# Two hybrid decoder layers on one core: planned weight conversions, attention in equal rounds from the second query slab on, a split last unit

## The chip, the cores and the metric

The kernel runs on one core of a Trainium2 chip. The metric is the device time of one execution in microseconds (us); lower is better. The engines are named as the profile names them: PE (TensorE matmul), PEld (its weight loads), DVE (VectorE), ACT (ScalarE), POOL (GpSimd), SP (SyncE, which issues nearly all DMAs).

## The reference

512 tokens of 1024 features go through two layers. Each layer projects the normalised tokens into an HGRN2 group (a gated linear recurrence, 8 heads) and a sliding-window attention group (16 query heads of 64, 2 key/value heads, window 128), and projects the joined, gated outputs back:

```python
def hybrid_layer(x, w_in, w_out, g_pre, g_post, lb, g_head, sinks):
    h = rms_norm(x, g_pre)
    proj = jnp.einsum('bsd,de->bse', h, w_in)
    q_h, f_h, i_h, z_h, q_a, k_a, v_a, z_a = jnp.split(proj, SPLIT_POINTS, axis=-1)
    o_h = hgrn2(q_h, f_h, i_h, lb)
    o_h = rms_norm(o_h, g_head).reshape(B, S, HG_WIDTH).astype(z_h.dtype) * jax.nn.silu(z_h)
    q_a = rotary(q_a.reshape(B, S, ATT_HEADS, ATT_HEAD_DIM), pos)
    k_a = rotary(k_a.reshape(B, S, ATT_KV_HEADS, ATT_HEAD_DIM), pos)
    o_a = sliding_window_attention(q_a, k_a, v_a, sinks).astype(z_a.dtype) * jax.nn.silu(z_a)
    y = jnp.einsum('bse,ed->bsd', jnp.concatenate([o_h, o_a], axis=-1), w_out)
    return x + rms_norm(y, g_post)
```

Attention works on blocks of 128 queries, each with its own and the previous block of keys, with a causal band of 128, a learned sink per head in the softmax, and rotated queries and keys. All data are float32.

## The kernel before

**Projections.** Every projection is made of three fp32r products of split operands (high x low, low x high, high x high), so each weight piece of 128 x 512 is converted after its load: ACT rounds it to `whi` (line 177), DVE, for some pieces POOL, subtracts that from it into `wlo` (line 178). Eight pieces make a *slab*. The slabs of a layer come in a fixed order: kv, two query slabs (QA), two of HGRN2's inputs (IV), then FQ (forget gates and queries), ZA (attention's gate), the output parts a0 and a1, FQ again, and so on to ZH, h0 and h1. Raw pieces have 4 buffers, converted ones 9 (`RAW_BUFS`, `W_BUFS`).

**Units and steps.** A slab is worked off in *units*, one output tile in the PSUM tag `pj` (3 buffers) each: four units of eight steps for an input slab, eight of four steps for an output part. A step is three matmuls of 128 x 512 (line 240). `step()` starts the next unit when none is active or the active one is half done, and then alternates between the two. When a unit starts, `w_conv` writes down the conversions of its whole slab; after each step it writes down as many pieces of the next slab as the step's share of this slab, and four more (`LEAD`). In the QA, FQ and ZA slabs a unit needs two of the eight pieces, in the others all eight.

**What sets the order.** `merge` interleaves a stream of other work with `step()` by shares of their totals; the scheduler of the tile framework then orders each engine's instructions by their dependences, by free buffers and by the place in the program. On the chip each engine runs its list in order.

**Attention.** A step of attention is a group of four heads (g = 0 to 3) and a block of queries (n = 0 to 3), 16 steps in all. `att_scores` needs one PSUM bank for n = 0 and two for the others out of three (`sc`, taken in turn): scores on PE (lines 474, 485), masking copy and maximum on DVE (477 to 490), `negm` and `ds` (493, 495), four exponentials on ACT that free the bank (499), sum and reciprocal on DVE, scaling on POOL (506). `att_transpose` follows two steps later (PE line 512, split on ACT and DVE, two selects on POOL, line 524), `att_value` four steps later (PE line 538, ACT 540, DVE 544). Each of the three counts 1 in `merge`, of a total of 50, against the 96 steps of IV, IV + 1 and the first FQ slab. It begins when all four groups of queries are there and two more steps are done.

**Queries.** `qa_stream` rotates a group on DVE (435 to 442) and POOL (445, 446), splits it (448, 449), writes it to DRAM (`stack`, line 451) and reads it back stacked (`qs`, four DMAs, line 454) into one of two buffers, all issued from SP, as the raw weight loads are.

**The end of a layer.** After each row tile's two units of h1, `final` adds up (776), squares (805), scales (807 on POOL, 810 on DVE), takes the root (296, 298) and adds the residual (813), and stores (814).

Of the kernel before, what the change touches and what calls it, by code (L numbers as in the profile page):

```python
# [19 lines left out]
DEPTH = 2  # L20
# [9 lines left out]
QA, IV, FQ, ZA, ZH = 0, 2, 4, 8, 10  # L30

# [3 lines left out]
VLAG = 4  # L35
DEFER = 18
PJ, SC = 3, 3
LEAD = 4
# [27 lines left out]
def hybrid_kernel(ctx: ExitStack, tc: tile.TileContext, x, wkv, win, wout, g_pre, g_post, lbp, ghead, sinks,  # L66
# [78 lines left out]
    ahead = {("kv", l): sum(slab_first["out", l - 1, "h1"]) for l in range(1, DEPTH)}  # L145
    for l in range(DEPTH - 1):
        ahead["out", l, "h1"] = sum(slab_first["out", l, "h1"]) - KT - LEAD
# [61 lines left out]
    class Unit:  # L209
        def __init__(self, key, ks, sta, mov, evac, needs, ncol):  # L210
            self.key, self.ks, self.sta, self.mov, self.evac, self.needs, self.ncol = key, list(ks), sta, mov, evac, needs, ncol
            self.i = 0
            self.fresh = key[0] == "kv"
            self.list = products(self.ks, self.fresh)

    units, active, turn, slab_steps, slab_done = deque(), [], [0], {}, {}

    def enqueue(key, specs, ncol=512):

        for ks, sta, mov, evac, needs in specs:  # L220
            units.append(Unit(key, ks, sta, mov, evac, needs, ncol))
            slab_steps[key] = slab_steps.get(key, 0) + len(units[-1].ks)
            slab_done.setdefault(key, 0)

    def step():
        if not active or (len(active) == 1 and units and not active[0].fresh and not units[0].fresh
                          and 2 * (len(active[0].ks) - active[0].i) <= len(active[0].ks)):
# [9 lines left out]
        turn[0] += 1  # L237
        for n in range(3 * u.i, 3 * u.i + 3):
# [8 lines left out]
        first, n = slab_first[u.key]  # L247
        w_conv(ahead.get(u.key, first + n) + slab_done[u.key] * KT // slab_steps[u.key] + LEAD)
# [125 lines left out]
    def layer(l, last):  # L374
# [51 lines left out]
        qs = {}  # L426

        def qa_stream(s):
            hold = {}

            def evac(m, o):
# [20 lines left out]
                st = big.tile([P, 4, 512], F32R, tag="b8", name="qs", bufs=2)  # L452
                for row, j, i in ((0, 1, 0), (32, 0, 1), (64, 0, 0), (96, 1, 1)):
                    nc.sync.dma_start(st[row:row + 32].bitcast(F32), stack[j, i].rearrange("(h p) t -> p h t", h=4))
                qs[g] = st
# [90 lines left out]
        def att_stream(steps):  # L546
            pts, terms = {}, {}
# [3 lines left out]
            for i in range(n + VLAG):  # L551
                if i < n:
                    until(lambda: steps[i][0] in qs)
                    pts[i] = att_scores(*steps[i])
                    yield 1.0
                if 2 <= i <= n + 1:
                    terms[i - 2] = att_transpose(*steps[i - 2], pts.pop(i - 2), i % 2)
                    yield 1.0
                if i >= VLAG:
                    att_value(*steps[i - VLAG], terms.pop(i - VLAG))  # L560
                    yield 1.0
# [206 lines left out]
        def wo_stream(b, s, final=None):  # L768
            def evac(o, tt, ch):
# [4 lines left out]
                else:  # L774
                    with tc.high_priority(200 if final else 0):
                        nc.vector.tensor_tensor(yt[tt][:, ch], o, yt[tt][:, ch], op=ALU.add)
                if final is not None:
                    final(tt, ch)

            enqueue(("out", l, f"{b}{s}"),  # L780
                    [(range(4 * ch, 4 * ch + 4), lambda k, w, tt=tt: tuple(t[:, k % 4, tt * P:(tt + 1) * P] for t in ops_t[b, s]),
                      lambda k, w: w[k], lambda o, tt=tt, ch=ch: evac(o, tt, ch), [("o", l, b, s, tt)])
                     for tt, ch in ([(tt, ch) for tt in range(NT) for ch in range(2)] if final else
# [245 lines left out]
```

## Time and profile before

| | us |
|---|---|
| median of three runs | 943.63 (943.48 to 945.7) |
| the profiled execution | 947.07 |
| its span | 945.3 |
| PE busy | 915.7 |
| DVE busy | 678.3 |
| ACT busy | 471.6 |
| POOL busy | 269.1 |

The span runs from the first instruction to the last; the execution's own time holds the launch beside it. In a row of instructions, the first two numbers are start and duration in us, then engine, line, operation, output<-inputs and shape; the bracket at the end is how long the engine stood idle before it, and what ended that. Matmul ends are modelled, so the pitch from start to start says more than a duration. In layer 0 attention runs from 75 us to 184 us, in layer 1 from 540 to 650; layer 1 begins at about 485.

### The profile page before, as it was taken

Reading aid. Unit: us, or ns where it says so; the run is one execution under the profiler, and the core shown is the slowest. Engines: PE = TensorE matmul, PEld = TensorE weight load, DVE = VectorE, ACT = ScalarE, POOL = GpSimd, SP = SyncE. Lnnn points to the kernel's source line nnn. Section 1 sums busy time; section 2 is a strip of 40 time slices with the busy share of each in tenths; the row PEclk is TensorE's granted clock in tenths of the full one; section 3 lists DMA queues with packets and bytes.
Section 4 is the critical chain, followed back from the end, with each engine's and each line's share of the span. In section 5 each row is a group of like instructions: output and inputs, shape, how many; then the busy total and the mean of one; then the engine's idle time right before and its main releaser. Section 6 shows DMA issues by size and latency. Waiting matters only on the chain.

```text
span 945.3 us, 19028 instructions
## 1 busy us (share of the span) xinstructions
PE 915.7 (97%) x7228; PEld 754.0 (80%) x7228; DVE 678.3 (72%) x1320; ACT 471.6 (50%) x1099; POOL 269.1 (28%) x287
## 2 busy tenths in 40 slices
PE   8999998999999999999989989989999999999996
PEld 6887887778878888788878878877787887887885
DVE  5886878786676784855787677878867677749446
ACT  4534766837364462434453266675463635425242
POOL 2423443422231221311232244432413213113102
PEclk9999999999999999999999999999999999999998
DMA  6475522222222232323356735222222233322313
GB/s 218 153 232 147 170 49 87 67 80 68 79 84 85 82 111 88 117 86 104 120 162 184 222 71 164 68 61 85 69 67 91 68 90 111 102 68 92 89 34 133
DMA packets 56427, 100.75 MB, mean 107 GB/s; under 512 B 6544, under 2 KB 8848, under 8 KB 56336
## 3 DMA queue, kind: packets, MB, share of 16 engines
q1 hardware_dynamic: 56048, 99.27, 34.9%
q8 instruction: 57, 0.93, 0.4%
q10 hardware_dynamic: 288, 0.27, 0.1%
q14 instruction: 34, 0.28, 0.1%
HBM read 86.93 MB, written 12.58 MB: 105 GB/s over the span
## 4 chain that ended last, share of the span: by engine, by line
PE 77%; DVE 9%; ACT 6%; issue 5%; POOL 2%; DMA 1%; DVEq 0%; POOLq 0%; SPq 0%; ACTq 0%
PE pj L240 64%; DVE wlo L178 3%; PE sc L640 2%; ACT s L499 2%; PE sc L485 2%; PE ac L709 2%; PE ac L697 1%; PE ac L538 1%; PE ac L712 1%; ACT whi L177 1%; DVE oa L544 1%; PE sc L757 1%; DVE mx L490 1%; PE sc L512 1%; PE sc L687 1%
## 5 line engine op out<-in xcount | busy, mean ns | idle before, releaser
L177 ACT CAST whi<-raw 128x512 fp32r<-128x512 f32 x256 | 157.8, 620 | 179.8 <-PE pj L240 159.8
L178 DVE TENSOR_TENSOR wlo<-raw,whi 128x512 fp32r<-128x512 f32 x249 | 189.0, 765 | 55.4 <-ACT whi L177 53.7
L240 PE MATMUL pj<-hhi,wlo 128*128 128x512 f32 x512 | 205.5, 401 | 0.0
L240 PE MATMUL pj<-hhi,whi 128*128 128x512 f32 x512 | 200.2, 391 | 0.0
L240 PE MATMUL pj<-hlo,whi 128*128 128x512 f32 x512 | 200.0, 391 | 0.0
L240 PE MATMUL pj<-whi,ops 128*128 128x512 f32 x512 | 173.5, 398 | 0.0
L240 PEld LDWEIGHTS pj<-hhi,whi 128*128 128x128 f32 x512 | 96.2, 188 | 20.9
L240 PEld LDWEIGHTS pj<-whi,ops 128*128 128x128 f32 x512 | 96.2, 188 | 19.9
L240 PEld LDWEIGHTS pj<-hhi,wlo 128*128 128x128 f32 x512 | 96.3, 188 | 19.0
L240 PEld LDWEIGHTS pj<-hlo,whi 128*128 128x128 f32 x512 | 96.5, 189 | 18.3
L240 PE MATMUL pj<-whi,hlo 128*128 128x512 f32 x256 | 104.6, 408 | 0.0
L240 PE MATMUL pj<-whi,hhi 128*128 128x512 f32 x256 | 101.0, 395 | 0.0
L240 PE MATMUL pj<-wlo,hhi 128*128 128x512 f32 x256 | 100.9, 394 | 0.0
L240 PE MATMUL pj<-wlo,ops 128*128 128x512 f32 x256 | 99.8, 390 | 0.0
L658 POOL TENSOR_TENSOR k<-k,tot 128x256 f32<-128x256 f32 x80 | 65.3, 835 | 109.6 <-PE sc L640 64.1
L657 DVE TENSOR_TENSOR q<-q,tot 128x256 f32<-128x256 f32 x80 | 48.2, 630 | 15.6 <-PE sc L640 10.1
L499 ACT ACTIVATE s<-sc,negm 128x128 f32<-128x128 f32 x128 | 45.6, 369 | 24.6 <-DVE negm L493 22.5
L240 PEld LDWEIGHTS pj<-whi,hhi 128*128 128x128 f32 x256 | 48.5, 189 | 10.2
L506 POOL TENSOR_TENSOR s<-s,sums 128x512 f32<-128x512 f32 x32 | 33.4, 1043 | 78.0 <-DVE sums L504 39.3
L240 PEld LDWEIGHTS pj<-wlo,ops 128*128 128x128 f32 x256 | 48.2, 188 | 8.9
L240 PEld LDWEIGHTS pj<-whi,hlo 128*128 128x128 f32 x256 | 48.6, 190 | 8.1
L240 PEld LDWEIGHTS pj<-wlo,hhi 128*128 128x128 f32 x256 | 48.7, 190 | 7.8
(182 smaller groups left out, 1431.5 us busy)
## 6 DMA issues: line engine op xcount, KB each, us to landing
raw<-in_win_dram SPq DMA_DIRECT2D x192, 256.0 KB, 2.7
raw<-in_wout_dram SPq DMA_DIRECT2D x64, 256.0 KB, 2.7
stack<-rot SPq DMA_DIRECT2D x16, 512.0 KB, 4.1
qs<-stack SPq DMA_DIRECT2D x32, 256.0 KB, 4.7
a<-in_x_dram SPq DMA_DIRECT2D x11, 256.0 KB, 3.6
raw<-in_wkv_dram SPq DMA_DIRECT2D x8, 256.0 KB, 4.0
x_mid<-a SPq DMA_DIRECT2D x8, 256.0 KB, 2.2
a<-x_mid SPq DMA_DIRECT2D x8, 256.0 KB, 3.0
```

The costliest lines, as they stand in the source:

```text
L177: keep(nc.scalar.copy(hi, v))
L178: keep((nc.gpsimd if i in on_pool and i % 2 else nc.vector).tensor_tensor(lo, v, hi.bitcast(F32), op=ALU.subtract))
L240: nc.tensor.matmul(u.o, lhsT=u.sta(k, u.w)[i], rhs=u.mov(k, u.w)[j], start=(n == 0), stop=(n == len(u.list) - 1))
L485: pin(nc.tensor.matmul(S[:, h * 256:(h + 1) * 256], lhsT=q[:, 2 * hp_ + h, t_], rhs=kst[v][p][:, (n - 1) * P:(n + 1) * P], start=(h == 0 a ...
L490: nc.vector.tensor_reduce(mx_[:, 2 * hp_:2 * hp_ + 2], Sv[:, :, P:2 * P], axis=AX.X, op=ALU.max)
L499: nc.scalar.activation(pt[:, h * P:(h + 1) * P], cur[h], AF.Exp, bias=negm[:, h:h + 1], scale=SCALE, accum_out=sums[:, h:h + 1])
L506: nc.gpsimd.tensor_tensor(pv, pv, sums.unsqueeze(2).broadcast_to([P, 4, P]), op=ALU.mult)
L512: pin(nc.tensor.transpose(T[:, h * P:(h + 1) * P], pt[:, h * P:(h + 1) * P], ident))
L640: pin(nc.tensor.matmul(L[32 * b:32 * b + 32, c:c + 16], lhsT=k[:, o_:o_ + 32], rhs=qv[:, blk:blk + qu, 1, :], start=True, stop=True, tile_ ...
L657: nc.vector.tensor_tensor(qv[:, :, 1, :], qv[:, :, 1, :], tv[:, :, 0].unsqueeze(2).broadcast_to([P, nb, hh]), op=ALU.mult)
L658: nc.gpsimd.tensor_tensor(kv_[:, :, 0, :], kv_[:, :, 0, :], tv[:, :, 1].unsqueeze(2).broadcast_to([P, nb, hh]), op=ALU.mult)
L709: pin(nc.tensor.matmul(O[:, c], lhsT=A[:, c], rhs=vs(j, n), start=(n == 0), stop=False))
```

## The change

- `plan_conversions` runs through all units once before the first step and notes at which step each weight piece is first used. Each piece is due 14 steps before that (`LEAD`), and at least 3 steps before the next piece (`SPACE`); `step()` writes down a conversion when it is due, or when a unit's step needs it. Nothing else is written down at a unit's start, and a step asks for its own pieces alone.
- Attention starts when two groups of queries are there and eight more steps are done (`QWAIT`), in the second QA slab. Its total is now 20, one for each round, and the one to three pieces of a round share that 1. The steps set against it are what is left of the second QA slab, IV, IV + 1 and the first FQ slab.
- The stacked queries of groups 2 and 3 are read back after the last score step of groups 0 and 1.
- The units of the last layer's h1 are not interleaved. Its last unit is split in two of 256 columns each, with its own sums, and the last row tile's stores go out in three parts, one of them from ACT's queue.

```diff
+    def begins(active, units):
+        return not active or (len(active) == 1 and units and not active[0].alone and not units[0].alone
+                              and 2 * (len(active[0].ks) - active[0].i) <= len(active[0].ks))
+    def plan_conversions():
+        first, on, rest, n = {}, [], deque(units), 0
+        while on or rest:
+            if begins(on, rest):
+                on.append(rest.popleft())
+            u = on[n % len(on)]
+            for j in u.pieces if u.fresh else [u.pieces[u.i]]:
+                first.setdefault(slab_first[u.key][0] + j, n)
...
+        for p in reversed(range(len(pieces))):
+            late = min(late, first[p] - LEAD) if p not in kv_pieces else late
+            due.insert(0, late)
+            late -= SPACE
...
     def step():
...
             u = units.popleft()
-            first, n = slab_first[u.key]
-            w_conv(first + n)
-            u.w = [conv[first + j] for j in range(n)]
...
+        for j in u.pieces if u.fresh else [u.pieces[u.i]]:
+            w_conv(first + j + 1)
+            u.w[j] = conv[first + j]
...
-        w_conv(ahead.get(u.key, first + n) + slab_done[u.key] * KT // slab_steps[u.key] + LEAD)
+        while state["conv"] < len(pieces) and due[state["conv"]] <= turn[0]:
+            n = state["conv"]
+            w_conv(n + 1)
+            if state["conv"] == n:
+                break
...
+        def load_q(g):
+            st = big.tile([P, 4, 512], F32R, tag="b8", name="qs", bufs=2)
+            for row, j, i in ((0, 1, 0), (32, 0, 1), (64, 0, 0), (96, 1, 1)):
+                nc.sync.dma_start(st[row:row + 32].bitcast(F32), stacks[g][j, i].rearrange("(h p) t -> p h t", h=4))
+            qs[g] = st
...
+                stacks[g] = stack
+                if g < 2:
+                    load_q(g)
...
             for i in range(n + VLAG):
+                todo = []
                 if i < n:
-                    until(lambda: steps[i][0] in qs)
-                    pts[i] = att_scores(*steps[i])
-                    yield 1.0
+                    todo.append(lambda: pts.update({i: att_scores(*steps[i])}))
...
+                for fn in todo:
+                    fn()
+                    yield 1.0 / len(todo)
+                if i < n and steps[i][1] == NT - 1 and steps[i][0] < 2:
+                    until(lambda: steps[i][0] + 2 in stacks)
+                    load_q(steps[i][0] + 2)
...
+                if last:
+                    todo[-1:] = [(NT - 1, 1, 0, 256), (NT - 1, 1, 256, 256)]
...
-            until(lambda: 3 in qs)
-            for _ in range(2):
+            until(lambda: 1 in qs)
+            for _ in range(QWAIT):
                 step()
-            merge((att_stream([(g, n) for g in range(4) for n in range(NT)]), 50), rest(("in", l, FQ)))
+            merge((att_stream([(g, n) for g in range(4) for n in range(NT)]), 4 * NT + VLAG), rest(("in", l, FQ)))
```

How the instructions stand, at three places. **PE, the first score steps of layer 0** (`sc` are the three banks, `ident,s` is the transpose of the first step). Before, with six, six, three and three projection matmuls at the gaps:

```order
L474 MATMUL sc_80<-kst,qs 128x128 x8
...
L485 MATMUL sc_78<-kst,qs 128x256 x4
L485 MATMUL sc_79<-kst,qs 128x256 x4
...
L485 MATMUL sc_80<-kst,qs 128x256 x4
...
L485 MATMUL sc_78<-kst,qs 128x256 x4
...
L512 MATMUL sc_79<-ident,s 128x128 x4
```

Now, with 18, three and six at the gaps:

```order
L520 MATMUL sc_80<-kst,qs 128x128 x8
L531 MATMUL sc_78<-kst,qs 128x256 x4
L531 MATMUL sc_79<-kst,qs 128x256 x4
...
L531 MATMUL sc_80<-kst,qs 128x256 x4
...
L531 MATMUL sc_78<-kst,qs 128x256 x4
...
L558 MATMUL sc_79<-ident,s 128x128 x4
```

The third step, which takes bank 80 again, stands 18 projection matmuls behind the second instead of six. The first stands 60 of them earlier in the program: 51 matmuls into the second QA slab, where before it stood 15 into IV. In both orders later steps are 18 matmuls apart.

**DVE, where the second QA slab ends and IV begins in layer 0** (`rot<-pj` are the rotations of the slab's last unit). Now:

```order
L325 TENSOR_TENSOR a<-sc_79,a 128x512
L488 TENSOR_TENSOR rot<-pj,cs 128x512
L177 TENSOR_TENSOR wlo<-raw,whi 128x512 x3
L489 TENSOR_TENSOR rot<-pj,cs 128x512
L177 TENSOR_TENSOR wlo<-raw,whi 128x512
L496 TENSOR_TENSOR rot<-rot 128x512
L523 COPY_PREDICATED sc_80<-masks,neg 128x512
```

Before:

```order
L178 TENSOR_TENSOR wlo<-raw,whi 128x512
L441 TENSOR_TENSOR rot<-pj,cs 128x512
L442 TENSOR_TENSOR rot<-pj,cs 128x512
L449 TENSOR_TENSOR rot<-rot 128x512 x2
L477 COPY_PREDICATED sc_80<-masks,neg 128x512
```

Before, all eight pieces of IV were converted ahead of the last rotation; now the fourth and later ones stand behind it, and four score steps stand ahead of it.

**DVE, a score step near the end of attention in layer 0** (from the masking copies to `negm`, on which the exponentials wait). Before, the 14th step, at the start of FQ:

```order
L544 TENSOR_TENSOR oa<-ac,u 64x2x128 x2
L178 TENSOR_TENSOR wlo<-raw,whi 128x512
L489 COPY_PREDICATED sc_80<-masks,sc_80 128x2x128
L489 COPY_PREDICATED sc_78<-masks,sc_78 128x2x128
L490 TENSOR_REDUCE mx<-sc_80 128x2
L178 TENSOR_TENSOR wlo<-raw,whi 128x512
L490 TENSOR_REDUCE mx<-sc_78 128x2
L284 TENSOR_TENSOR a<-sc_79,a 128x512
L178 TENSOR_TENSOR wlo<-raw,whi 128x512
L493 SCALAR_TENSOR_TENSOR negm<-mx,nsnk 128x4
```

Now, the 15th, at the end of IV + 1:

```order
L590 TENSOR_TENSOR oa<-ac,u 64x2x128 x2
L535 COPY_PREDICATED sc_80<-masks,sc_80 128x2x128
L535 COPY_PREDICATED sc_78<-masks,sc_78 128x2x128
L536 TENSOR_REDUCE mx<-sc_80 128x2
L536 TENSOR_REDUCE mx<-sc_78 128x2
L177 TENSOR_TENSOR wlo<-raw,whi 128x512
L539 SCALAR_TENSOR_TENSOR negm<-mx,nsnk 128x4
```

One conversion is left in this chain where there were three. Before, the last score step stands 36 matmuls into FQ, now nine. ACT's list has 18 table loads instead of 22.

More of the change, by code (lines that the diff above doesn't have):

```diff
@@ L35 @@
 VLAG = 4
+QWAIT = 8
 DEFER = 18
 PJ, SC = 3, 3
-LEAD = 4
+LEAD, SPACE = 14, 3
 POOL_SLABS = (QA,)
@@ L225, in step @@
     def step():
-        if not active or (len(active) == 1 and units and not active[0].fresh and not units[0].fresh
-                          and 2 * (len(active[0].ks) - active[0].i) <= len(active[0].ks)):
+        if not due:
+            plan_conversions()
+        if begins(active, units):
             u = units.popleft()
-            first, n = slab_first[u.key]
-            w_conv(first + n)
-            u.w = [conv[first + j] for j in range(n)]
             for key in u.needs:
```

84 lines of the change are left out of this document (55 added, 29 removed).

## The prediction

> **What bounds the kernel now.** I read the page first, then the table of waits of the tensor engine, then busy time by stage, then the timeline of single stalls.
>
> ```profile
> span 945.3 us, 19028 instructions
> PE 915.7 (97%) x7228; PEld 754.0 (80%) x7228; DVE 678.3 (72%) x1320; ACT 471.6 (50%) x1099; POOL 269.1 (28%) x287
> ```
>
> The tensor engine (PE) is busy for 97% of the span, and the change adds twelve matmuls and removes none. So it can only win back PE's idle time, time at a reduced clock, and what follows the last matmul. Of the waits, one is large:
>
> ```profile
> PE sc L485 <- ACT s L499: 11.5, 11, 2.6
> ```
>
> The score matmuls of attention (line 485) wait for the exponentials (line 499) that free one of the three score banks. By stage (columns: stretch, its length, then busy us and count of PE, PEld, DVE, ACT, POOL, then PE's granted clock, DMA share, GB/s), three stretches of each layer hold most of it:
>
> ```profile
> 75.00:90.00 15.00, 12.98 (x68) 10.91 (x67) 10.54 (x29) 7.52 (x32) 4.77 (x5) 0.89 0.25 95
> 90.00:105.00 15.00, 14.58 (x82) 12.12 (x81) 12.82 (x29) 9.74 (x36) 9.35 (x9) 1.00 0.55 149
> 150.00:165.00 15.00, 12.45 (x67) 10.29 (x66) 13.02 (x31) 9.65 (x30) 4.88 (x5) 1.00 0.23 73
> 540.00:555.00 15.00, 12.83 (x64) 10.73 (x63) 11.46 (x32) 8.67 (x33) 3.52 (x4) 0.89 0.12 44
> 555.00:570.00 15.00, 14.33 (x76) 11.51 (x75) 13.15 (x28) 10.50 (x37) 9.03 (x9) 1.00 0.63 169
> 615.00:630.00 15.00, 12.46 (x61) 10.43 (x60) 11.66 (x29) 8.43 (x27) 4.61 (x4) 0.89 0.24 71
> ```
>
> Length less PE busy is the idle time: at attention's start 2.02 + 0.42 us in layer 0 and 2.17 + 0.67 in layer 1, near its end 2.55 and 2.54. Three of the stretches show a clock of 0.89: 15 us x 0.11 = 1.65 us lost at most; since part of the slow time falls into the stall itself I take 1.4 each.
>
> **Start of attention.** What ended the first stall, with PE's pitch ahead of it:
>
> ```profile
> 77.66 1.12 PE L485 MATMUL sc<-kst,qs 128*128 128x256 f32 x8
> 78.61 0.40 PE L240 MATMUL pj<-whi,hlo 128*128 128x512 f32 x1
> ...
> 79.55 0.39 PE L240 MATMUL pj<-wlo,hhi 128*128 128x512 f32 x1
> 79.78 0.39 PE L240 MATMUL pj<-whi,hhi 128*128 128x512 f32 x1
> 82.18 0.51 PE L485 MATMUL sc<-kst,qs 128*128 128x256 f32 x2 [2.02 <-ACT s L499]
> ```
>
> Projection matmuls follow each other every 0.23 us; eight score matmuls take 78.61 - 77.66 = 0.95. The third score step comes six projection matmuls after the second, too soon for the exponentials of the first. The order after the change puts 18 there: twelve more, 12 x 0.23 = 2.8 us, over the 2.02 and 2.17 that were missing. So this stall and its slow clock should go: 2.02 + 0.42 + 1.4 = 3.8 in layer 0, 2.17 + 0.67 + 1.4 = 4.2 in layer 1, 8.1 in all.
>
> But attention now starts inside the second query slab, where VectorE (DVE) also rotates queries. From the first score to that slab's end, PE has 54 projection matmuls x 0.23 = 12.4 us, four score steps at 0.95 and two transposes of half the columns of a score step at about 0.4: 17 us. DVE's work there, counted in its new order, by these groups (line, op, count, total us, mean ns) of the attention stage of layer 0, and a rotation and a conversion ahead of it:
>
> ```profile
> L284 DVE TENSOR_TENSOR a<-sc,a 128x512 fp32r<-128x512 f32 x16 | 11.0, 686 | 1.1 <-ACT a L283 0.5
> L489 DVE COPY_PREDICATED sc<-masks,sc 128x256 f32<-128x256 uint8 x24 | 9.7, 422 | 3.7 <-PE sc L485 1.5 <-ACT a L283 1.1 <-ACT whi L177 0.9
> L490 DVE TENSOR_REDUCE mx<-sc 128x2 f32<-128x256 f32 x24 | 9.6, 418 | 0.2
> L503 DVE TENSOR_TENSOR sums<-sums,es 128x4 f32<-128x4 f32 x16 | 5.5, 341 | 9.5 <-ACT es L502 9.5
> ```
>
> ```profile
> 63.93 0.68 DVE L442 TENSOR_TENSOR rot<-pj,cs 128x512 f32<-128x512 f32 x1
> 64.53 1.41 DVE L178 TENSOR_TENSOR wlo<-raw,whi 128x512 fp32r<-128x512 f32 x1
> ```
>
> Eight masking copies and eight maxima (the full-width one as two) 8 x (0.42 + 0.42) = 6.7; sixteen small ones at up to 0.34, 5.4; two transposed subtracts 1.4; four rotations 2.7; two rounding subtracts of that width and one conversion at up to 1.41, 4.2: 20.4 us. With the small ones at 0.15, as line 296 below, and those three at 0.68, it is 15.2. DVE is thus as full as PE. The next slab's fourth and later conversions stand behind the last rotation in DVE's queue, and PE's first unit of IV waits for them. The lower count gives PE no stall; the upper, (20.4 + 0.95 until the first score is there - 17) + rotation 0.68 + conversion 0.68 - (0.95 + 0.23 of PE work ahead of it), a stall of 4.5. I take 1.5 per layer, below the middle, since the group means lie nearer to their short ends. **Term A: -8.1 + 3.0 = -5.1, ends +0.9 and -8.1.**
>
> The DMAs move too:
>
> ```profile
> 51.54 1.27 SPq L454 DMA_DIRECT2D qs<-stack  x3
> ...
> 72.78 0.99 SPq L157 DMA_DIRECT2D raw<-in_win_dram  x1
> 89.40 1.75 SPq L454 DMA_DIRECT2D qs<-stack  x4
> ```
>
> SP stands from 73.8 to 89.4 on the read-back of the third stack, since both buffers are in use, with the raw weight loads behind it. The change issues that read-back when its buffer is nearly free. PE shows no wait for a weight there, so I cost the gain at nothing. The first score needs the first stack's read-back:
>
> ```profile
> 75.36 0.33 PE L474 MATMUL sc<-kst,qs 128*128 128x128 f32 x2
> ```
>
> ```profile
> qs<-stack SPq DMA_DIRECT2D x32, 256.0 KB, 4.7
> ```
>
> That score moves ahead by 60 projection matmuls, 13.8 us, to 61.6; the last part of the read-back, issued by 52.8, lands 4.7 later at 57.5. The 4 us between hide it; without them PE would wait for what is missing, at most one landing.
>
> **End of attention.** The second stall of layer 0, the conversions that DVE did in the 4 us ahead of it (count, shortest, median and longest in ns, first and last start), and a table load:
>
> ```profile
> 155.81 0.73 PE L485 MATMUL sc<-kst,qs 128*128 128x256 f32 x4 [2.56 <-ACT s L499]
> ```
>
> ```profile
> L178 DVE TENSOR_TENSOR wlo<-raw,whi x3: 676/676/996, 149.8 to 153.3; 128x512 fp32r<-128x512 f32 x3
> ```
>
> ```profile
> 161.32 1.28 ACT L583 ACT_TABLE_LOAD   x1
> ```
>
> Here the eight weight pieces of the first FQ slab are converted at once, three of them inside the chain copy, maximum, negm on which the exponentials wait: 0.68 + 0.68 + 1.00. In the new order one is left, so the chain is shorter by 1.7 of the 2.55. The scores also end 9 matmuls into FQ instead of 36, and four loads of the exponential or sigmoid table go, 4 x 1.28 us of ScalarE, which is off PE's path except here. I take -1.7 in layer 0 and -1.7 - 1.4 (the slow clock) in layer 1. **Term B: -4.8, ends 0 and -6.5** (2.55 + 2.54 + 1.4).
>
> **The tail.** DVE behind PE's last matmul:
>
> ```profile
> 936.60 0.69 DVE L776 TENSOR_TENSOR y<-pj,y 128x512 f32<-128x512 f32 x1 [0.27 <-PE pj L240]
> 937.33 1.71 DVE L810 TENSOR_TENSOR s<-y,b 128x512 f32<-128x512 f32 x1
> 938.96 0.15 DVE L296 SCALAR_TENSOR_TENSOR s<-ss 128x1 f32<-128x1 f32 x1
> 939.76 0.75 DVE L813 SCALAR_TENSOR_TENSOR a<-y,r,a 128x512 f32<-128x512 f32 x1 [0.66 <-POOL r L298]
> 940.43 0.74 DVE L813 SCALAR_TENSOR_TENSOR a<-s,r,a 128x512 f32<-128x512 f32 x1
> ```
>
> From 936.60, when PE's last matmul is done, to DVE's last end, 941.17, is 4.6 us. Now half a unit comes last, at about 0.42 for a half-width operation (line 490's size): y 0.4, square and its sum on ScalarE about 0.6, then 0.15 and the 0.8 to line 813, then 0.67 + 2 x 0.42: 3.3 us. The multiply of line 810, drawn out to 1.71 beside POOL's, is no longer there at the end, since the units now run one after the other and the first half-row is done 2.7 us earlier. Against it, 24 matmuls of 256 columns at 0.95 / 8 = 0.119 in place of 12 at 0.23 cost 0.1. **Term C: -1.2, ends -0.5 and -1.5.** The rest, the conversions shifted elsewhere and the seam between the layers: 0, plus or minus 1.5: no wait of PE there is in the table beside the one above, and the conversions run under PE's matmuls on engines that are busy for 72% and 50%; without that cover each would cost PE its 0.68.
>
> Sum: -5.1 - 4.8 - 1.2 = -11.1. The profiled execution took 947.07 us with a span of 945.3; the span would be 934.2. The median of the runs, 943.63, lies below that execution, and against it I predict **932.5 us**.
>
> **Two rules against the change.** The rotation's POOL part began just ahead of the conversion quoted above, and this stood beside POOL's selects:
>
> ```profile
> 64.09 1.29 POOL L445 TENSOR_TENSOR rot<-rot 128x512 f32<-128x512 f32 x1 [7.41 <-DVE rot L441]
> ```
>
> ```profile
> 153.87 1.04 DVE L493 SCALAR_TENSOR_TENSOR negm<-mx,nsnk 128x4 f32<-128x4 f32 x1
> ```
>
> The conversion took 1.41 instead of 0.68, and negm 1.04, where line 296 took 0.15 for as much. The Trainium skill, page "SBUF — State Buffer", section "Who interferes with whom", says why: a VectorE instruction with two SBUF inputs and a GpSimd one that reads SBUF exclude each other for the whole instruction. By that rule attention beside the rotations is worse than either alone; the case is the slower rival below. The clock: the Trainium skill, page "TensorE: Matmul & The Clock Gate", section "What's actually happening", halves it after an idle window of about 3.4 us; by that the three slow stretches would not exist, and the sum would be -6.9. Here 2.02 us sufficed, and the stall of 2.56 ahead of 155.81 did not: the windows' 0.89 and 1.00 decide.
>
> **Rivals.** *One of the two stalls stays.* The nine weight buffers and three banks are unchanged, IV's pieces still bunch at IV's end, and the late scores still pass there; or DVE in the query slab returns all of A. Against: the new orders at both places. A + C = -6.3 gives 937.3, B + C = -6.0 gives 937.6: 937.5. *All stalls vanish:* -8.1 - 6.5 - 1.2 = -15.8, 927.8; against it, DVE's full queue. *Only the tail gains,* since both stalls reappear: 942.4. *Slower:* in the query slab most DVE instructions with two SBUF inputs meet POOL: eight of its twelve small ones at 1.04 instead of 0.15 (+7.1), two rounding subtracts and a conversion at 1.41 instead of 0.68 (+2.2): 9.3 us of stall per layer. 2 x 9.3 - 8.1 - 4.8 - 1.2 = +4.5: 948.1. It decides from 7.1 us per layer. Against: POOL's work there, four rotation steps at 1.29 and the scaling of four rounds, leaves it idle for a third of the 17 us or more. *That the change doesn't do what it says* is excluded by the orders.
>
> **Chances.** Forecast 0.47; one stall stays 0.26; all vanish 0.12; tail only 0.09; slower 0.06. About 0.3% (2.8 us) is what a measurement of this kernel can tell from no change: faster, below 940.8, is 0.47 + 0.26 + 0.12 = 0.85; same 0.09; slower 0.06. The range, 925.5 to 941, leaves out the last two cases and the extreme of the third.
>
> **What would show it.** Right: the wait of line 485's matmuls for the exponentials falls from 11.5 to about 2 to 4 us; the windows at attention's start show a clock of 1.00; PE has a gap of 1 to 3 us per layer ahead of IV's first unit, released by DVE's conversion; 18 table loads; from the last matmul to DVE's end 3.3 us. Wrong: gaps of over 7 us per layer in the second query slab with DVE full; stalls of 2.5 us still at FQ's start; PE waiting for the query read-back or a raw weight.

## The result, and the profile after the change

| | before | after | ratio, 95% interval |
|---|---|---|---|
| first comparison, median | 943.86 us (943.48 to 945.70, 4 executions) | **937.74 us** (937.65 to 938.35, 4 executions) | 0.9926 [0.9911, 0.9941] |
| repeated beside three experiments | 945.95 us (943.77 to 947.64, 9 executions) | 937.71 us (937.44 to 938.64, 4 executions) | 0.9910 [0.9897, 0.9924] |
| profiled execution | 947.07 us, span 945.3 | 937.74 us, span 936.0 | |

The change makes the kernel faster by 6.1 us in the first comparison and by 8.2 in the repeated one. The forecast was 932.5, 11.1 us less than before; the measured 937.74 is 5.2 us above it and lies inside the range of 925.5 to 941. The kernel before spreads over more than 4 us and the changed one over 1; why is the subject of the first experiment.

The page of the changed kernel, first the span and the busy time of each engine:

```profile
span 936.0 us, 18967 instructions
PE 911.8 (97%) x7240; PEld 754.2 (81%) x7240; DVE 673.5 (72%) x1324; ACT 461.5 (49%) x1097; POOL 270.2 (29%) x287
```

Its table of waits of the tensor engine (what waited, for what, us in total, times, longest):

```profile
PE pj L278 <- DVE wlo L177: 4.6, 4, 2.0
PE sc L531 <- ACT s L545: 2.8, 6, 0.7
```

The score matmuls (now line 531) wait 2.8 us for the exponentials instead of 11.5. A wait that was not there now leads the table: projection matmuls that wait for the low part of a converted weight piece, 4.6 us. Busy time in the stretches that the prediction read (columns as there: length, PE, PEld, DVE, ACT, POOL, then PE's granted clock, DMA share, GB/s):

```profile
75.00:90.00 15.00, 13.10 (x60) 10.38 (x60) 12.61 (x22) 7.46 (x23) 7.96 (x6) 0.89 0.32 105
90.00:105.00 15.00, 13.66 (x70) 10.86 (x69) 12.75 (x32) 8.63 (x35) 6.91 (x7) 1.00 0.65 177
150.00:165.00 15.00, 15.00 (x79) 12.62 (x78) 11.93 (x31) 11.25 (x32) 6.83 (x7) 1.00 0.35 106
540.00:555.00 15.00, 12.31 (x58) 9.77 (x57) 13.70 (x24) 8.91 (x27) 9.12 (x8) 0.89 0.58 190
555.00:570.00 15.00, 15.00 (x78) 12.40 (x77) 11.44 (x30) 9.07 (x35) 5.03 (x5) 1.00 0.47 108
615.00:630.00 15.00, 15.00 (x76) 12.49 (x75) 9.54 (x20) 11.39 (x26) 7.08 (x8) 1.00 0.21 68
```

At attention's end (third and last row) PE has no idle time left: 2.55 and 2.54 us are gone. In the stretches where attention started before, PE idles 1.90 + 1.34 us in layer 0 and 2.69 + 0 in layer 1, 5.9 in all, where it was 5.3; the reduced clock is there too. Attention now starts earlier, and in the stretches ahead, 60 to 75 and 525 to 540, where PE had no idle time before, it idles 0.61 and 0.80 us: 7.3 in all. So the stall at the start did not go. It changed its cause.

Where the 9.3 us between the two spans lie is read from two marks that both kernels have: the last transpose of layer 1's first norm, and PE's last matmul. Of the kernel before, on PE's timeline:

```profile
485.24 0.60 PE L343 MATMUL sc<-ident,xn 128*128 128x128 f32 x4
936.17 0.39 PE L240 MATMUL pj<-whi,ops 128*128 128x512 f32 x1
```

and of the changed kernel:

```profile
483.36 0.60 PE L384 MATMUL sc<-ident,xn 128*128 128x128 f32 x4
928.14 0.28 PE L278 MATMUL pj<-whi,ops 128*128 128x256 f32 x1
```

Up to the seam the change gains 1.9 us, from there to the last matmul 450.9 - 444.8 = 6.1, and behind the last matmul 9.1 - 7.9 = 1.3.

### The profile page after: what moved, and what is told of

It is laid out like the page before. It is cut to its first block, busy times and chain, and to the rows that moved or that the text cites. A ratio compares the mean times of both kernels' runs of the same rounds, so it can differ in the third digit from the quotient of the medians.

```text
span 936.0 us, 18967 instructions
## 1 busy us (share of the span) xinstructions
PE 911.8 (97%) x7240; PEld 754.2 (81%) x7240; DVE 673.5 (72%) x1324; ACT 461.5 (49%) x1097; POOL 270.2 (29%) x287
## 4 chain that ended last, share of the span: by engine, by line
PE 84%; DVE 8%; ACT 3%; issue 2%; POOL 1%; DMA 1%; SPq 0%; POOLq 0%; DVEq 0%; ACTq 0%
PE pj L278 70%; PE sc L692 2%; PE ac L584 2%; PE sc L531 2%; DVE wlo L177 2%; PE ac L761 2%; PE ac L764 1%; PE ac L749 1%; ACT s L545 1%; PE sc L558 1%; PE sc L809 1%; POOL r L339 1%; PE sc L739 1%; DVE a L885 1%; PE sc L703 1%
## 5 line engine op out<-in xcount | busy, mean ns | idle before, releaser
L176 ACT CAST whi<-raw 128x512 fp32r<-128x512 f32 x256 | 154.8, 622 | 89.2 <-PE pj L278 67.2
L278 PE MATMUL pj<-whi,ops 128*128 128x512 f32 (+1 forms) x520 | 173.5, 395 | 0.0
L278 PE MATMUL pj<-wlo,ops 128*128 128x512 f32 (+1 forms) x260 | 100.5, 387 | 0.0
L709 DVE TENSOR_TENSOR q<-q,tot 128x256 f32<-128x256 f32 x80 | 52.6, 689 | 17.3 <-PE sc L692 9.5
L552 POOL TENSOR_TENSOR s<-s,sums 128x512 f32<-128x512 f32 x32 | 35.9, 1121 | 59.0 <-ACT a L324 30.1
```

Of the source, the lines that this page charges most:

```text
L176: keep(nc.scalar.copy(hi, v))
L278: nc.tensor.matmul(u.o, lhsT=u.sta(k, u.w)[i], rhs=u.mov(k, u.w)[j], start=(n == 0), stop=(n == len(u.list) - 1))
L552: nc.gpsimd.tensor_tensor(pv, pv, sums.unsqueeze(2).broadcast_to([P, 4, P]), op=ALU.mult)
L709: nc.vector.tensor_tensor(qv[:, :, 1, :], qv[:, :, 1, :], tv[:, :, 0].unsqueeze(2).broadcast_to([P, nb, hh]), op=ALU.mult)
```

## The experiments

Each time is a median; the ratio, with its interval, is to the kernel before, timed beside it on the same chip. The tail, the conversions, attention and the last two together were timed in one session (before 945.75), the three around the new wait with the changed kernel in a second (945.95), and later attention, the conversions on GpSimd and the last kernel in a third (944.51).

**The tail alone.** The kernel before with the tail's edits; attention and conversions as they were:

```
+todo[-1:] = [(NT - 1, 1, 0, 256), (NT - 1, 1, 256, 256)]
+self.alone = self.fresh or key == ("out", DEPTH - 1, "h1")
+(nc.scalar if split and i == 1 else nc.sync).dma_start(...)
```

> The kernel before with the last part of the change alone: the units of the last slab run one after the other, its last unit is two halves, and three stores close the program. Conversions and attention stay as they were. By my sum (term C): 1.2 us less than before, ends 0.5 and 1.5, so about 942.5; last matmul to DVE's last end 3.3 us instead of 4.6. By a rival, that the store's landing sets the end and is merely issued from two queues: within 0.4 us of before.

Measured: 944.22 us, ratio 0.9986 [0.9975, 0.9997]: by the ratio 1.3 us less, with an interval from 0.3 to 2.4. The sum's size, but not its reason, as the rows of the tail show. VectorE behind PE's last matmul in the changed kernel, whose tail is the same:

```profile
928.72 0.78 DVE L868 TENSOR_TENSOR ss<-ss 128x1 f32<-128x1 f32 x1 [0.60 <-ACT u L871]
929.43 0.41 DVE L829 TENSOR_TENSOR y<-pj,y 128x256 f32<-128x256 f32 x1
929.87 0.43 DVE L878 TENSOR_TENSOR s<-y,b 128x256 f32<-128x256 f32 x1
930.47 0.16 DVE L337 SCALAR_TENSOR_TENSOR s<-ss 128x1 f32<-128x1 f32 x1 [0.17 <-ACT u L871]
931.29 0.75 DVE L885 SCALAR_TENSOR_TENSOR a<-y,r,a 128x512 f32<-128x512 f32 x1 [0.66 <-POOL r L339]
931.96 0.87 DVE L885 SCALAR_TENSOR_TENSOR a<-s,r,a 128x256 f32<-128x256 f32 x2
```

From the last y (929.43) to VectorE's end (932.83) it is 3.4 us, as forecast (3.3). But that y starts 1.29 us behind the start of PE's last matmul; before it was 936.60 - 936.17 = 0.43. Ahead of it in VectorE's queue stands line 868, which adds up two partial sums of squares and waits for ScalarE's square of the first half. So from PE's last matmul's start to VectorE's end only 0.3 us is gained (5.0 to 4.7). The rest of the 1.3 us between the profiles, 1.0, lies behind VectorE's end: 4.15 us in the profile before, 3.2 after. The profiles of the four experiments below that keep the whole last unit have 3.0 to 3.1 there, so a split unit is not needed for that. With the attention and the conversions of the change, the tail's edits gain nothing: the medians are 937.47 without them and 937.74 or 937.71 with them. So the edits are worth about 1 us beside the kernel before and nothing in the changed one; of the first only 0.3 is accounted for, and why the two differ stays open.

This run shows something else, more important for the forecast. Its attention is that of the kernel before, stalls included. Two of them, on PE's timeline:

```profile
82.38 0.73 PE L523 MATMUL sc<-kst,qs 128*128 128x256 f32 x4 [2.02 <-ACT s L537]
...
544.90 0.74 PE L523 MATMUL sc<-kst,qs 128*128 128x256 f32 x4 [2.16 <-ACT s L537]
```

The stretches around the three stalls, first in the kernel before, then in this one (granted clock third from the end):

```profile
80.00:90.00 10.00, 7.98 (x38) 6.70 (x38) 7.21 (x25) 6.27 (x30) 2.23 (x3) 0.83 0.00 0
545.00:555.00 10.00, 8.71 (x42) 7.52 (x43) 6.74 (x22) 6.50 (x31) 3.12 (x3) 0.83 0.05 16
615.00:625.00 10.00, 7.46 (x33) 6.15 (x32) 8.23 (x19) 3.46 (x16) 3.56 (x3) 0.83 0.27 80
```

```profile
80.00:90.00 10.00, 7.98 (x47) 6.48 (x46) 8.65 (x28) 6.33 (x31) 3.12 (x3) 1.00 0.09 22
543.00:553.00 10.00, 8.10 (x40) 7.06 (x41) 6.74 (x22) 6.84 (x32) 2.61 (x3) 0.83 0.01 4
614.00:624.00 10.00, 7.43 (x40) 6.03 (x39) 8.72 (x21) 5.18 (x22) 3.56 (x3) 1.00 0.26 80
```

The same stalls, and the clock drops behind all three in one execution and behind one in the other. Each drop takes the same 10 x 0.17 = 1.7 us of clock. In time, one costs 1.4 us there: the last transpose of layer 1's first norm, at 485.24 us in the kernel before, stands at 483.87 in this one, whose first layer has no drop, 1.4 us earlier. How many drops an execution has differs, and the times of the kernel before fall into groups accordingly. All 52 executions of it that ran beside the experiments:

| mean granted clock | executions | us, lowest, median, highest |
|---|---|---|
| 0.996 | 19 | 943.3, 943.9, 944.5 |
| 0.993 and 0.994 | 21 | 945.4, 945.9, 946.4 |
| 0.992 | 12 | 947.1, 947.3, 947.7 |

0.002 of 944 us is 1.9, about one such drop. The profiled execution (947.07, clock 0.992) is of the last group, with three drops; the median of the three times shown ahead of the prediction, 943.63, lies by its time in the first, whose clock says two fewer; the median of all 52 is 945.8. The tail kernel's twelve executions fall into the same groups (one at 0.995 taken with 0.994), with medians of 942.9, 944.8 and 946.2, 1.0 to 1.1 us below the kernel before in each.

**The conversions alone, and attention alone.** Conversions alone: planning as in the change, attention's start, its 50-step share and the read-back of the stacks as before. Attention alone: the other way round.

```
conversions alone, against the kernel before:
-w_conv(ahead.get(u.key, first + n) + slab_done[u.key] * KT // slab_steps[u.key] + LEAD)
+while state["conv"] < len(pieces) and due[state["conv"]] <= turn[0]:
...
attention alone, against the kernel before:
-until(lambda: 3 in qs)
-for _ in range(2):
+until(lambda: 1 in qs)
+for _ in range(QWAIT):
...
-merge((att_stream([(g, n) for g in range(4) for n in range(NT)]), 50), rest(("in", l, FQ)))
+merge((att_stream([(g, n) for g in range(4) for n in range(NT)]), 4 * NT + VLAG), rest(("in", l, FQ)))
```

> The kernel before with the planned conversions alone (each weight piece 14 steps ahead of its first use, 3 steps apart); attention starts late and is dealt as before, the tail is whole. Theory 1 (the conversions in the chain copy, maximum, negm make the stall at attention's end): 3 to 5 us less than before, the two gaps of 2.5 us at the fourth FQ slab's start gone; the two gaps at attention's start (2.0 and 2.2) stay. Theory 2 (those gaps come from scores that are dealt too thick there, and from where they end): under 1 us less, the gaps stay.

> The kernel before with the attention part alone (start in the second query slab, 20 equal rounds, late read-back of two stacks); each unit's eight pieces are converted by the old rule, the tail is whole. Theory 1: the score wait at attention's start goes (6.9 us with its slow clock less what the new stall costs), but with the old rule all eight pieces of the first IV slab stand behind the rotation, so the stall there is at least that of the changed kernel (2.3 us per layer on a wait for the conversions): 0 to 5 us less than before. Theory 2 (the stall at IV has nothing to do with how conversions are planned, only with attention beside the rotations): as much gained as conversions and attention together.

> The changed kernel with the old tail. If the tail is worth the 1.2 us of my sum and adds to the rest, 1.2 us more than the changed kernel, about 4.9 us less than before: 939. If attention and conversions only pay together, this is more than the sum of what each is worth alone; if they take the same stalls away, less.

Measured: conversions alone 942.61, ratio 0.9968 [0.9955, 0.9981]; attention alone 947.73, 1.0026 [1.0016, 1.0036], which is *slower* than before; both without the tail 937.47, 0.9920 [0.9904, 0.9936]. In medians -3.1, +2.0 and -8.3: seven us of the gain belong to neither part but to the two together. For the conversions, theory 1 named the time and the end of the two gaps of 2.5 us, but the gaps at attention's start, which it had stay, went too. Neither theory foresaw that attention alone would lose, and the wait for conversions that theory 1 expected there is not in its table of waits.

Conversions alone take away the score wait nearly whole (1.2 us left of 11.5), and PE idles all the same. The wait that leads there is for the probabilities that GpSimd scales, here with its longest pause:

```profile
PE sc L553 <- POOL s L547: 3.1, 3, 1.9
```

```profile
105.13 0.66 PE L553 MATMUL sc<-ident,s 128*128 128x128 f32 x4 [1.87 <-POOL s L547]
```

The pause of 1.87 us is a transpose's, 23 us behind the old stall; the 2.03 us of idle time from 165 to 180 us are three pauses of 0.70, 1.02 and 0.31, the longest for VectorE's line 585. That attention's rounds, still dealt unevenly, make the next engine in the chain late is argued from this. The two changes also do not part cleanly at attention's start: the program starts it as before, but the first score stands at 80.61 us with the conversions alone instead of 75.36, behind the last rotation, and what that does is the subject of the next experiment. The nine executions with the conversions alone have a mean clock of 0.996 to 0.998, against 0.992 to 0.996 before; at 0.996 in both they are 0.8 us faster, so most of the 3 us is clock. Compared at equal clock in the same way, attention alone loses 1.8 and both together gain 8.6.

Attention alone has a stall that is longer than the one it should remove. PE, and VectorE ahead of it:

```profile
92.56 1.23 PE L528 MATMUL sc<-kst,qs 128*128 128x256 f32 x4 [3.42 <-ACT s L542]
```

```profile
85.21 2.55 DVE L493 TENSOR_TENSOR rot<-rot 128x512 fp32r<-128x512 f32 x2 [0.45 <-ACT rot L492]
87.68 0.68 DVE L322 TENSOR_TENSOR a<-sc,a 128x512 fp32r<-128x512 f32 x1
88.28 0.68 DVE L180 TENSOR_TENSOR wlo<-raw,whi 128x512 fp32r<-128x512 f32 x1
88.88 0.74 DVE L520 COPY_PREDICATED_SCALAR sc<-masks,neg 128x512 f32 x1
```

The mask of a score step whose matmuls began at 84.37 starts at 88.88, behind the last rotation's two subtracts (2.55 us for two that took 0.68 each when undisturbed), a transposed subtract and a conversion. The kernel before has the same at the start of its attention, on VectorE's timeline, with the first score's matmuls at 75.36:

```profile
76.99 1.95 DVE L449 TENSOR_TENSOR rot<-rot 128x512 fp32r<-128x512 f32 x2 [1.50 <-ACT rot L448]
78.86 0.75 DVE L477 COPY_PREDICATED_SCALAR sc<-masks,neg 128x512 f32 x1
```

So the stall there may come, too, not from score steps that are too close, as the prediction had it, but from one that meets the end of the query slab. Starting attention earlier then only lets another step meet it.

**Attention later in the kernel before.** This tests that reading with one number:

```
 until(lambda: 3 in qs)
-for _ in range(2):
+for _ in range(8):
```

> The kernel before with one number changed: attention starts 8 steps behind the fourth query stack instead of 2, so 18 projection matmuls (4.1 us) later. Theory 1 (the stall at attention's start comes from the last rotation: in the kernel before, the first score's masking copy starts at 78.86, behind the rotation's two subtracts, though the score itself starts at 75.36): the gaps of 2.0 and 2.2 us go, and the slow stretches set off by them: 4 to 6 us less than before. Theory 2 (as the prediction has it: score steps only six projection matmuls apart are too close for the exponentials): the stall moves with the scores and stays, within 1 us of before.

Measured: 945.23, ratio 0.9999 [0.9989, 1.0009]. Both expectations are half right: theory 1 has the cause, theory 2 the time. The start, with the mask of the first score step, whose matmuls begin at 79.53:

```profile
75.00:90.00 15.00, 15.00 (x84) 12.57 (x83) 9.98 (x29) 8.13 (x33) 4.65 (x4) 1.00 0.50 186
```

```profile
80.57 0.75 DVE L477 COPY_PREDICATED_SCALAR sc<-masks,neg 128x512 f32 x1 [1.55 <-PE sc L474]
```

PE is full there. The third score step comes seven projection matmuls behind the second, nearly as close as the six of the kernel before, and waits for nothing; the mask now starts 1.0 us behind its score, not 3.5. So the rotation made the stall of 2.02, and not the distance of the steps. But the time did not get shorter, since other pauses take the stall's place. The longest of layer 0, and a stretch around it:

```profile
100.67 0.74 PE L485 MATMUL sc<-kst,qs 128*128 128x256 f32 x4 [1.91 <-ACT s L499]
```

```profile
100.00:105.00 5.00, 4.33 (x16) 3.60 (x17) 4.87 (x12) 2.32 (x9) 1.11 (x2) 0.69 0.22 57
```

A later step waits 1.91 us for the exponentials, with a drop of the clock behind it. Behind attention's end, from 195 to 210 us, VectorE is full and PE idles 1.35 us instead of 0.23: the later end falls into the stage behind. From 75 to 210 us PE idles 6.4 us in all, where it was 6.3. That a stall at the start is won only where attention also ends earlier, and that the parts pay together for this reason, fits these figures and is not shown by them alone.

**The new wait: place or load.** In the changed kernel the fourth piece of IV is late. VectorE's conversions, GpSimd beside them, and PE:

```profile
81.56 4.68 DVE L177 TENSOR_TENSOR wlo<-raw,whi 128x512 fp32r<-128x512 f32 x3
```

```profile
81.42 1.10 POOL L570 TENSOR_SCALAR_AFFINE_SELECT pcur<-a 128x1024 fp32r<-128x1024 f32 x1
82.47 1.54 POOL L570 TENSOR_SCALAR_AFFINE_SELECT pprev<-a 128x1024 fp32r<-128x1024 f32 x1
83.98 1.71 POOL L492 TENSOR_TENSOR rot<-rot 128x512 f32<-128x512 f32 x1
```

```profile
83.12 0.50 PE L278 MATMUL pj<-wlo,hhi 128*128 128x512 f32 x1 [1.37 <-DVE wlo L177]
```

The three conversions stand directly behind the first multiply of the last rotation, where the order shown with the change has them. They take 1.56 us each instead of 0.68, while GpSimd works without a break. The Trainium skill, page "SBUF — State Buffer", section "Who interferes with whom", has VectorE and GpSimd lock each other out of a shared pair of ports; the trace agrees, since the third of them ends at 86.2, half a microsecond after GpSimd pauses. Three kernels try to take the wait away, each with one or two numbers changed, and one runs the changed kernel again beside them:

```
first:
-LEAD, SPACE = 14, 3
+LEAD, SPACE = 26, 3
second:
-QWAIT = 8
+QWAIT = 20
third:
-QWAIT = 8
+QWAIT = 20
-LEAD, SPACE = 14, 3
+LEAD, SPACE = 20, 3
```

> The changed kernel itself, beside the kernel before and the three below. Theory (slow clock comes in pieces of 1.7 us, each set off by a stall, and their number differs from execution to execution): the changed kernel has two of them in nearly every execution, after the stalls of the first IV units, so its times lie close together; the kernel before has one to three, so its times lie in steps of about 1.7 us. Expected 937.7, ratio 0.991 to 0.993.

> The changed kernel with each conversion due 26 steps ahead of its first use instead of 14: the fourth and later pieces of the first IV slab then stand ahead of the second query slab's last rotation on VectorE and between the exponentials on ScalarE. Theory 1 (the stall of the first IV units is the conversions' place in the queues): the wait of 4.6 us for the conversions goes, with the two slow stretches of 1.7 us that follow it: 8 us less, about 929.7. Theory 2 (VectorE is full in the query slab, so the work only changes places): the wait turns into one for the exponentials of about the same length, 936 to 939.

> The changed kernel with attention started 20 steps behind the second query stack instead of 8, so later by 36 matmuls (8 us), the 20 rounds dealt over the rest. Theory 2 (VectorE's load in the query slab makes the stall): less attention there, so the wait for the conversions shrinks to 1 us or less and the slow stretches go: 5 to 8 us less, if the rounds, 15 per cent closer together, don't bring the score wait back (then 936 to 941). Theory 1 (place in the queue): the conversions still stand behind the last rotation, the wait stays at 3 to 5 us.

> Both: attention 20 steps behind the second stack, conversions due 20 steps ahead. If either cause alone makes the stall, as good as the better of the two; if both are needed, better than each: below 930.

| attention starts behind the second stack by | conversions due ahead by | us | ratio to before |
|---|---|---|---|
| 8 steps (the change) | 14 | 937.71 | 0.9910 [0.9897, 0.9924] |
| 8 | 26 | 940.32 | 0.9938 [0.9924, 0.9951] |
| 20 | 14 | 938.33 | 0.9913 [0.9900, 0.9927] |
| 20 | 20 | 936.65 | 0.9897 [0.9884, 0.9911] |

Earlier conversions alone end the wait and cost 2.6 us: the wait has become one for the exponentials, as theory 2 said, and 940.3 is more than either theory expected.

```profile
PE sc L531 <- ACT s L545: 7.6, 6, 4.0
```

The later start cuts the wait for VectorE's conversions to 0.7 us, and score waits of 4.1 and 2.5 us take its place; in the timed executions nothing is gained. With both, 1.1 us are, far from the 930 expected if both causes were needed.

The changed kernel's second profile answers a further question: what the reduced clock costs there. Of four executions one had a mean clock of 0.998 and took 937.44; the others had 0.993 and 0.994 and took 937.65, 937.78 and 938.64. The second profile is that of 938.64. Its first layer has no drop at all. The same stretch in the first profile and in the second, and then the second's layer 1:

```profile
80.00:95.00 15.00, 12.44 (x57) 9.68 (x56) 14.81 (x22) 8.41 (x22) 9.45 (x7) 0.89 0.65 206
```

```profile
80.00:95.00 15.00, 11.24 (x58) 8.28 (x57) 14.85 (x21) 8.37 (x22) 9.48 (x7) 1.00 0.63 204
```

```profile
540.00:555.00 15.00, 13.01 (x53) 10.02 (x52) 13.93 (x24) 8.89 (x28) 8.88 (x7) 0.77 0.56 187
```

As many matmuls (57 and 58) in the same 15 us, at a clock of 0.89 and at 1.00. VectorE is full, 14.8 of 15 us; PE waits for it, and at the lower clock it only waits less. The last transpose of layer 1's first norm is no earlier without the drop, 483.58 us against 483.36. In layer 1 the second profile has a drop of twice the length (15 x 0.23 = 3.45 us of clock against 1.65), and from that transpose to the last matmul it is 0.7 us slower. So the single drops, which cost 1.4 to 2.0 us each in the kernel before, cost next to nothing here, and the long one a part of what it took.

**Conversions on GpSimd.** Every second subtract of the first IV slab moves from VectorE to GpSimd, in the changed kernel and in the one with 20 and 20:

```
-POOL_SLABS = (QA,)
+POOL_SLABS = (QA, IV)
```

> The changed kernel with the rounding subtract of every second piece of the first IV slab on GpSimd instead of VectorE. If VectorE's queue makes the wait of 4.6 us for the conversions (three of them behind the last rotation), half of them leave it: the wait falls to 1 to 3 us, 2 to 4 us less in all. If ScalarE's casts are late (they stand behind the third round's exponentials and start at 80.20), or if GpSimd is as late with them beside its rotation and its selects, nothing is gained: within 1 us of 937.7.

> The kernel with 20 and 20 that took 936.65, with every second subtract of the first IV slab on GpSimd. What is left there of waits for conversions is 0.9 us on VectorE and 0.7 on ScalarE; the score waits of 6.5 us come from VectorE's chain in the dense rounds, which loses four conversions per layer at 0.68: up to 2.7 us per layer less if they were all in that chain, so 931 to 936; if the freed time falls where PE does not wait, 936 to 937.

Measured: 939.47, 0.9936 [0.9922, 0.9951], in the changed kernel, 1.8 us worse than it and outside what was expected; 936.72, 0.9907 [0.9889, 0.9924], in the other, as good as without. PE now waits for GpSimd, whose conversions stand between its selects:

```profile
PE pj L278 <- POOL wlo L177: 5.9, 3, 2.6
```

```profile
82.44 1.70 POOL L177 TENSOR_TENSOR wlo<-raw,whi 128x512 fp32r<-128x512 f32 x1
84.09 1.54 POOL L570 TENSOR_SCALAR_AFFINE_SELECT pprev<-a 128x1024 fp32r<-128x1024 f32 x1
```

**Between the two.** The last kernel starts attention 14 steps behind the second stack and has conversions due 20 steps ahead:

```
-QWAIT = 8
+QWAIT = 14
-LEAD, SPACE = 14, 3
+LEAD, SPACE = 20, 3
```

> The changed kernel with attention 14 steps behind the second stack and conversions due 20 steps ahead: between the changed kernel and the one with 20 and 20 that took 936.65. If the later start is what helps, because less of VectorE's attention work meets the rotations, between 936.7 and 937.7; if the earlier conversions are, and the denser rounds cost, below 936.6.

Measured: **930.57 us** (929.87 to 930.67), ratio 0.9838 [0.9821, 0.9856]: 7.1 us less than the change. By its time it falls under the second expectation, below 936.6, but neither foresaw such a gain: it beats both neighbours by 6 us and more. Its stretch at the start of IV, and the number of conversions on VectorE between 50 us and 81 us, there and in the changed kernel:

```profile
75.00:90.00 15.00, 15.00 (x82) 12.49 (x81) 13.03 (x29) 8.36 (x28) 8.15 (x7) 1.00 0.36 125
```

```profile
L177 DVE TENSOR_TENSOR wlo<-raw,whi x6: 675/680/1327, 49.8 to 67.5; 128x512 fp32r<-128x512 f32 x6
```

```profile
L177 DVE TENSOR_TENSOR wlo<-raw,whi x4: 677/681/1406, 49.4 to 66.1; 128x512 fp32r<-128x512 f32 x4
```

Two more pieces are converted before the last rotation, PE has 82 matmuls there in place of 60 and no idle time, and the clock stays at 1.00 in every stretch up to the last matmul. Which of the two numbers does it is not shown: neither was run alone at these values, and the neighbours at 8 and 14, 8 and 26, and 20 and 20 are all 6 us or more behind, which suggests that it hangs on where single steps meet, not on a trend.

## Why the prediction was right and wrong

**Right in sign and range, too large in size.** Of the 5.2 us between 932.5 and 937.74, 3.4 come from the yardstick and 1.8 from the sum.

**The yardstick.** The step that failed is "the median of the runs, 943.63, lies below that execution, and against it I predict". The sum was made on an execution of 947.07 with three clock drops and took credit for all three, 3 x 1.4 = 4.2. The median it was set against has, by its clock, two fewer, so two drops were saved twice. 947.07 - 11.1 would have been 936.0. A drop's size was right: 1.4 was taken, and the groups of the kernel before lie 2.0 and 1.4 apart.

**Term A (attention's start): -5.1 forecast.** The place of the new stall was right, the fourth IV piece behind the last rotation, and its size not: 4.6 us for both layers instead of 3.0. The price of 0.68 per conversion was the mis-sized factor; beside GpSimd it was 1.56. PE's idle time at the start went from 5.3 to 7.3 us, where the sum had 3.0. What the term still gained is the clock: in the windows it is at 0.89 as before, against the forecast of 1.00, but it costs next to nothing there. The explanation of the old stall ("the third score step comes six projection matmuls after the second, too soon") was wrong: with steps as close, behind the rotation, it was gone, and the rotation was the cause. The slow conversions and small operations beside GpSimd, at 1.41 and 1.04 in the prediction's own rows, were in the upper end of its stall and in the slower rival; the sum took 1.5 per layer, below the middle of 0 and 4.5, and the middle is what the wait came to, 2.3.

**Term B (attention's end): -4.8 forecast.** Larger: both stalls are gone whole, 2.55 + 2.54, and with them the profiled execution's drop of 1.4, -6.5, which was the term's far end. That the conversions in the chain are the reason is not shown: attention alone, with the old rule, ends that stall too. Its stretches:

```profile
150.00:165.00 15.00, 14.58 (x76) 12.13 (x75) 12.65 (x32) 9.89 (x31) 5.48 (x6) 1.00 0.45 136
615.00:630.00 15.00, 14.58 (x78) 11.86 (x77) 12.41 (x28) 9.92 (x34) 6.07 (x6) 1.00 0.44 122
```

Together, A and B came to 1.9 + 6.1 = 8.0 for the two layers with all else in them, against 9.9. The layers differ. In layer 0, 1.4 of the 1.9 are the drop that the profile before had there. In layer 1 PE's idle time from 525 to 675 us fell by 2.9, from 6.7 to 3.8, and one drop went, 1.4 to 1.7; at least 1.5 of the 6.1 are not accounted for.

**Term C (tail): -1.2 forecast.** Timed alone it agrees, -1.3, but in the changed kernel the same edits gained nothing, and inside the profile only 0.3 us are accounted for: the merge of the partial sums, which the working left out, stands ahead of the last y and waits 0.60 for ScalarE.

**The score wait** was forecast at 2 to 4 us and is 2.8; the sum had taken 8.7 of 11.5 from it, and 8.7 went. The table loads are 18 as forecast.

**The rivals.** What happened is nearest to the first, "VectorE in the query slab returns all of A", and its 937.6 matches the median for the wrong reason, since it went by the same yardstick. The slower rival has the sign of what attention alone does, at stalls of 3.42 and 2.62 us instead of the 9.3 per layer that it named. Treating the parts as terms that add was the deeper fault: -3.1 and +2.0 alone became -8.3 together.

## What to carry to other kernels

A stall that a busy engine causes moves when the work is moved: before counting it as won, say which instruction is late next, and whether the stage also ends earlier; and follow it through the whole stage, not only to where it stood. Make the sum and the reference time from executions with the same granted clock, or count only what both contain. And when an engine's work is pushed beside another that shares its memory ports, price it by the disturbed rows of the trace.

## What the runs showed of the hardware

A stall of the same length is followed by a drop of PE's granted clock in one execution and not in the next: 2.02 us without and 2.16 with, in the same execution of the tail kernel, and 2.02 with in the kernel before. From 83 to 87 us the kernel before has a clock of 0.56, 0.50, 0.50 and 0.73 in stretches of 1 us. Each such drop takes 10 us x 0.17, which is 3.4 us at half the clock. The Trainium skill, page "TensorE: Matmul & The Clock Gate", section "What's actually happening", gives the clock two values, full and half, and a free-running window of about 3.4 us; both values and the length agree, but for the one drop of twice the length. Its condition of a whole idle window does not: a single pause of 1.91 us was enough in the kernel with later attention, and one of 2.56 was not in the kernel before. That the phase of the window against the stall decides is argued from this, not shown.

A drop costs time where PE is the bound: 1.4 to 2.0 us in the kernel before, next to nothing behind the new stall, where VectorE was.
